# A hybrid decoder block with product-key experts on one core: operands of the gate products kept token by token

## The chip, the cores and the metric

The kernel runs on one core of one Trainium2 chip, in one launch. The metric is device time in microseconds (us), from the start to the end of one execution; a few executions are timed and the median is quoted. One further execution is recorded by the hardware profiler, and the rows below come from that one. Engines are called as the profile calls them: PE (TensorE, matmuls), PEld (the weight loads of PE), DVE (VectorE), ACT (ScalarE), POOL (GpSimd) and SP (SyncE, which here issues DMAs).

## The reference

One decoder layer on 512 tokens of width 1024: modulation from `c`, an attention group (8 query heads, window 128, sinks) beside a gated short convolution, an output projection, and then a product-key expert layer, which takes most of the time. Cut to that layer:

```python
q  = (xt @ wq).reshape(T, 8, 2, 128)
sc = einsum('thpd,hpkd->thpk', q, subkeys)          # 8 heads, two halves, 128 keys
vals, ids = lax.top_k(sc, 16)                       # per half
cand = vals[..0, :, None] + vals[..1, None, :]      # 256 candidates a head
top, pos = lax.top_k(cand, 16)
idx = take(ids0 * 128 + ids1, pos);  g = softmax(top)
for tokens in chunks of 128:                        # u, v: 16384 x 1024 each
    a   = einsum('chkd,cd->chk', u[idx], x)
    out = einsum('chk,chkd->cd', g * gelu(a), v[idx])
```

Each token thus picks 128 of 16384 experts (8 heads, 16 each), every one of which is a row of `u` and a row of `v` of 1024 floats. An expert's number is 128 i + j, with i and j from 0 to 127.

## The kernel before

**Two ways through the experts.** Of the 512 tokens, 384 (`TD`) are worked densely: all 16384 experts are multiplied out on PE, 128 at a time (one slice j holds the 128 experts of all i), and those that a token did not pick get gate zero. The last 128 tokens gather their rows of `u` and `v` by indirect DMAs on POOL and take dot products and sums on DVE (`gathered`, lines 771, 779, 894). 64 of the 384 dense tokens (`HT`) gather their rows of `u` too (`last_dense`), so that the first dense product has 320 columns (`TU`).

**First product (`first`, line 608 on).** For slice j the table `uL[j]` (512 KB) is loaded, split into two reduced-precision parts by ACT (`hi`, line 174) and DVE (`lo`, line 175), and multiplied in 24 matmuls of 320 columns (lines 198 to 200); ACT writes the gelu (line 619). Results of the first 64 slices (`SPILL`) go to DRAM, a pair of slices at a time (`Ad`, 320 KB), and come back as `sp`. Those of the other slices wait on the chip, in `RING` = 5 buffers `ge` of one pair each.

**Gates (`build`, lines 903 to 944).** The dense gates of 16 tokens are built at a time, in 24 builds. For each token, PE multiplies a 128x128 matrix A (row = one of the token's 128 picks, 1 where i matches) with B (row = pick, value = gate where j matches), once for the gate's upper part (B1, line 938) and once for its lower (B2, line 939). The product is the token's 128x128 map of gates. DVE makes A by comparing with an iota (line 926), and B as the product of two smaller matrices, H (the upper three bits of j) and L1 or L2 (the lower four bits, times the gate; lines 920 to 923 and 930). H, L, L1 and L2 are made for two builds at once. The operands are float16, in tiles laid out [4 groups][128 columns][4 tokens]: the 128 columns of one token lie 4 elements apart, and four neighbouring elements belong to four tokens. A matmul of one token reads `A[:, b, :, t]` and `B1[:, b, :, t]`. Four tokens share a PSUM bank, which ACT writes to `st` (line 941); after two builds `st` goes to DRAM (`Gd`, 2 MB).

**The loop around it.** Each build of the first 16 is followed by two `first` and three steps of `last_dense` (a row to fetch and a dot product on DVE); the last 8 builds by one `first` each. Then come the `first` still missing up to slice 72, and then the main loop over the 128 slices: `gated` loads the gates of 8 slices from `Gd` (`G`), multiplies them with the first product (line 963) and splits the result; `second` multiplies with `vL[j]` (18 matmuls of 512 columns, lines 980 to 982) into six PSUM banks that stay open to the end; from slice 64 on each slice has a further `first`. Steps of `gathered` are taken between, as many as `PACE` allows (1.85 us a slice before slice `SPILL`, 4.4 us from it on).

**What sets the order.** Every engine works its own queue in order; a scheduler puts the program's instructions into the queues by the order in which it is written and by data dependences. A tile with one or two buffers makes its writer wait for the readers of the earlier contents: A, B1 and B2 have two buffers, H, L, L1 and L2 one.

Of the kernel before, what the change touches and what calls it, by code (L numbers as in the profile page):

```python
# [9 lines left out]
F16 = mybir.dt.float16  # L10
# [3 lines left out]
AF = mybir.ActivationFunctionType  # L14
OP = mybir.AluOpType
# [3 lines left out]
P = 128  # L19
# [5 lines left out]
TD = ND * P  # L25
# [7 lines left out]
TB = 32  # L33
NB = TD // TB
GS = 32768.0
RING = 5
LOOK = 4
SPILL = 64
EARLY = 1
STB = 2  # L40
LD = 5
# [48 lines left out]
def body(tc, p):  # L90
    nc = tc.nc
    es = ExitStack()

    def pool(name, bufs=1, **kw):
        st = ExitStack()
        return st.enter_context(tc.tile_pool(name=name, bufs=bufs, **kw)), st

    cp, cp_s = pool("cp")
# [11 lines left out]
    def bank(name):  # L110
        return psm.tile([P, 512], F32, tag="m", name=name)
# [21 lines left out]
    nc.vector.memset(eps, EPS)  # L133
    eps64 = cp.tile([P, 1], F32, name="eps64")
    nc.vector.memset(eps64, 64 * EPS)
    iotaX = cp.tile([P, P, 4], F16, name="iotaX")
    nc.vector.tensor_copy(iotaX, C("iota")[:, :, None].to_broadcast([P, P, 4]))
    iotaA = cp.tile([P, 16, 16], F16, name="iotaA")
    nc.vector.tensor_copy(iotaA, C("iota")[:, 0:16, None].to_broadcast([P, 16, 16]))

# [336 lines left out]
    for step in PLAN.split():  # L477
        n = [int(x) for x in step[1:]]
# [75 lines left out]
    pp, pp_s = pool("pp")  # L554
    h2H = pp.tile([P, DC, TU], F32R, name="h2H")
    h2L = pp.tile([P, DC, TU], F32R, name="h2L")
    iT = pp.tile([P, TD], F16, name="iT")
    jhT = pp.tile([P, TD], F16, name="jhT")
    jlT = pp.tile([P, TD], F16, name="jlT")
    g1T = pp.tile([P, TD], F16, name="g1T")  # L560
    g2T = pp.tile([P, TD], F16, name="g2T")
    h2N = pp.tile([P, D], F32, name="h2N")
    hN = pp.tile([P, D], F32, name="hN")
    eH = pp.tile([P, HT], I32, name="eH")
# [18 lines left out]
    for r, (dst, cs) in enumerate(((hN, slice(TU - HT, TD)), (h2N, slice(TD, T)))):  # L583
        pg = [bank("pg0"), bank("pg1")]
        for k in range(DC):
            b = mod[:, 24 + k:25 + k]
# [15 lines left out]
    rp, rp_s = pool("rp", side="right")  # L602
    Ad = dp.tile([SPILL // 2, P, 2, TU], F32, name="Ad")
    ring = {}
    lead = [0]

    def first():
        j = lead[0]
        if j == NJ:
            return  # L610
        lead[0] += 1
        w = weights_of(p["uL"][j])
        ps = psa.tile([P, TU], F32, tag="a", name="pa")
        mm3(ps, w, lambda k: h2H[:, k, :], lambda k: h2L[:, k, :])
        m, i = divmod(j, 2)
        if i == 0:
            ring[m] = up.tile([P, 2, TU], F32, name="sp", bufs=3) if j < SPILL else \
                rg.tile([P, 2, TU], F32, name="ge", bufs=RING)
        nc.scalar.activation(ring[m][:, i], ps, AF.Gelu_apprx_tanh)  # L619
        if i and j < SPILL:  # L620
            nc.sync.dma_start(Ad[m], ring.pop(m))
# [201 lines left out]
    for c in range(ND):  # L823
# [11 lines left out]
        n = P if c < ND - 1 else P - HT  # L835
# [65 lines left out]
    stage, low = [None], [None]  # L901

    def build(bt):

        ts_ = slice(bt * 16, (bt + 1) * 16)

        def tok(x, w, ts):
            n = (ts.stop - ts.start) // 4
            return x[:, ts].rearrange("p (b t) -> p b t", t=4)[:, :, None, :].to_broadcast([P, n, w, 4])

        def iotas(step, w, n):
            return iotaX[:, None, 0:step * w:step, :].to_broadcast([P, n, w, 4])

        def tile_(name, n, w):
            return gb.tile([P, n, w, 4], F16, tag=name, name=name, bufs=1 if n == 8 else 2)

        if bt % 2 == 0:
            t2 = slice(bt * 16, (bt + 2) * 16)
            H, L, L1, L2 = [tile_(x, 8, w) for x, w in (("H", 8), ("L", 16), ("L1", 16), ("L2", 16))]
            nc.vector.tensor_tensor(H, iotas(16, 8, 8), tok(jhT, 8, t2), op=OP.is_equal)  # L920
            nc.vector.tensor_tensor(L, iotas(1, 16, 8), tok(jlT, 16, t2), op=OP.is_equal)
            nc.vector.tensor_mul(L1, L, tok(g1T, 16, t2))
            nc.vector.tensor_mul(L2, L, tok(g2T, 16, t2))
            low[0] = H, L1, L2
        A, B1, B2 = [tile_(x, 4, P) for x in ("A", "B1", "B2")]
        nc.vector.tensor_tensor(A, iotas(1, P, 4), tok(iT, P, ts_), op=OP.is_equal)
        bs = slice((bt % 2) * 4, (bt % 2) * 4 + 4)
        sh = [P, 4, 8, 16, 4]
        for B, L in ((B1, low[0][1]), (B2, low[0][2])):
            nc.vector.tensor_mul(B.rearrange("p b (h l) t -> p b h l t", h=8),  # L930
                                 low[0][0][:, bs, :, None, :].to_broadcast(sh), L[:, bs, None, :, :].to_broadcast(sh))
        if bt % 2 == 0:
            stage[0] = gb.tile([P, NJ, TB], F32, tag="st", name="st", bufs=STB)
        for b in range(4):
            ps = bank("gps")
            for t in range(4):
                o = ps[:, t * P:(t + 1) * P]
                nc.tensor.matmul(o, A[:, b, :, t], B1[:, b, :, t], start=True, stop=False)  # L938
                nc.tensor.matmul(o, A[:, b, :, t], B2[:, b, :, t], start=False, stop=True)  # L939
            t0 = (bt % 2) * 16 + b * 4  # L940
            nc.scalar.activation(stage[0][:, :, t0:t0 + 4], ps.rearrange("p (t j) -> p j t", t=4), AF.Copy,
                                 scale=1.0 / GS)
        if bt % 2:
            nc.sync.dma_start(Gd[bt // 2], stage[0])

    def gated(m):

        if 2 * m < SPILL:
            a = up.tile([P, 2, TU], F32, name="sp", bufs=3)
# [52 lines left out]
    gb, gb_s = pool("gb")  # L1002
# [110 lines left out]
```

## Time and profile before

| | us |
|---|---|
| median of 3 runs | 1490.91 (1484.22 to 1491.93) |
| the profiled execution | 1482.77 |
| its span, first to last instruction | 1481.0 |
| PE busy, in the span | 1414.3 |
| PEld busy | 1236.0 |
| DVE busy | 1268.3 |
| ACT busy | 613.8 |
| POOL busy | 439.2 |
| the 24 builds, first to last gate matmul | 480.4 to 703.5 |
| main loop, first multiplication of gates | 722.6 |

The profiled execution is 8.1 us shorter than the median of the timed runs. A matmul's row shows its start and a modelled length that overlaps the next one; how fast PE goes is therefore read from the distance of two starts, not from the length. [...] DMA is the mean busy share of the 16 DMA engines.

### The profile page before, as it was taken

What the parts mean: (1) busy time and instruction counts of PE and PEld (TensorE: products, weight loads), DVE (VectorE), ACT (ScalarE), POOL (GpSimd) and SP (SyncE); (2) the same over time, 40 slices, a digit from 0 to 9 for tenths busy, and PEclk for the clock granted to TensorE, in tenths of its full rate; (3) what the DMA queues carried; (4) which work ended last, traced back from release to release, by engine and by line L of the source; (5) the groups of instructions that cost most, each with busy time, mean ns of one, the idle gap of its engine ahead of it and who ended that gap; (6) DMA issues with size and microseconds to landing.
All of it is one profiled execution on the core that took longest, in us unless ns stands there. A gap on an engine that the chain in (4) does not pass through costs nothing.

```text
span 1481.0 us, 21313 instructions
## 1 busy us (share of the span) xinstructions
PE 1414.3 (95%) x7696; PEld 1236.0 (83%) x7696; DVE 1268.3 (86%) x2330; ACT 613.8 (41%) x1029; POOL 439.2 (30%) x324
## 2 busy tenths in 40 slices
PE   6999998999896999999999999998999999999998
PEld 4776776788896999999977888887888999888986
DVE  7777978899997899869789788887979999888984
ACT  4533546433632444544434433343333343433341
POOL 0000000000154033300122344454766655555600
PEclk9999999999998999999999999999999999999999
DMA  8644535232699599977898999999999999999963
GB/s 293 222 160 152 182 128 181 83 95 76 193 358 350 211 347 380 364 280 258 298 377 290 353 377 394 403 370 350 356 393 356 408 401 388 401 347 379 372 216 128
DMA packets 138282, 432.07 MB, mean 292 GB/s; under 512 B 13120, under 2 KB 39872, under 8 KB 136640
## 3 DMA queue, kind: packets, MB, share of 16 engines
q1 hardware_dynamic: 92096, 262.92, 49.3%
q0 software_dynamic: 46080, 167.79, 30.0%
q8 instruction: 60, 0.98, 0.3%
q14 instruction: 46, 0.38, 0.1%
HBM read 390.78 MB, written 39.85 MB: 291 GB/s over the span
## 4 chain that ended last, share of the span: by engine, by line
PE 23%; issue 9%; DMA 9%; DVE 7%; POOL 4%; ACT 0%; DVEq 0%; POOLq 0%
PE o L982 6%; PE o L981 5%; PE o L980 5%; DMA row<-in_uR,eG 4%; POOL row L771 4%; DMA row<-in_vL,eG 4%; PE pa L198 2%; PE pa L200 2%; PE pa L199 2%; DVE lo L175 2%; DVE ga L894 2%; DVE junk L779 1%; DVE wwl L175 1%; DVE x L999 0%; PE gps L939 0%
## 5 line engine op out<-in xcount | busy, mean ns | idle before, releaser
L174 ACT ACTIVATE hi<-raw 128x1024 fp32r<-128x1024 f32 x298 | 312.2, 1054 | 330.6 <-PE pa L199 153.5
L175 DVE TENSOR_TENSOR lo<-raw,hi 128x1024 fp32r<-128x1024 f32 x298 | 362.7, 1219 | 43.7 <-ACT hi L174 40.9
L198 PE MATMUL pa<-h2H,hi 128*128 128x320 f32 x1024 | 320.9, 313 | 17.8 <-ACT sp L619 17.8
L200 PE MATMUL pa<-h2H,lo 128*128 128x320 f32 x1024 | 320.2, 313 | 5.5 <-DVE lo L175 5.5
L199 PE MATMUL pa<-h2L,hi 128*128 128x320 f32 x1024 | 318.9, 311 | 0.0
L981 PE MATMUL o<-lo,wwh 128*128 128x512 f32 x768 | 301.4, 392 | 7.9 <-DVE lo L175 7.9
L982 PE MATMUL o<-hi,wwl 128*128 128x512 f32 x768 | 300.6, 391 | 4.5 <-DVE wwl L175 4.4
L980 PE MATMUL o<-hi,wwh 128*128 128x512 f32 x768 | 300.9, 392 | 0.0
L771 POOL DMA_INDIRECT row<-in_uR,eG x128 | 181.8, 1420 | 297.4 <-PE o L982 139.5
L771 POOL DMA_INDIRECT row<-in_uR,eH x64 | 83.0, 1298 | 553.9 <-DVE eq L690 407.2
L198 PEld LDWEIGHTS pa<-h2H,hi 128*128 128x128 f32 x1024 | 194.7, 190 | 21.7 <-ACT sp L619 19.5
L771 POOL DMA_INDIRECT row<-in_vL,eG x128 | 174.2, 1361 | 122.1 <-DVE ga L894 67.9
L779 DVE SCALAR_TENSOR_TENSOR junk<-row,h2N 128x1024 bf16<-128x1024 f32 x128 | 153.5, 1220 | 59.0 <-DMA row<-in_uR,eG 58.6
L200 PEld LDWEIGHTS pa<-h2H,lo 128*128 128x128 f32 x1024 | 194.3, 190 | 7.0 <-DVE lo L175 7.0
L199 PEld LDWEIGHTS pa<-h2L,hi 128*128 128x128 f32 x1024 | 194.4, 190 | 2.2
L894 DVE SCALAR_TENSOR_TENSOR ga<-row,av,ga 128x1024 f32<-128x1024 f32 x127 | 163.1, 1284 | 19.7 <-DMA row<-in_vL,eG 18.2
L981 PEld LDWEIGHTS o<-lo,wwh 128*128 128x128 f32 x768 | 144.8, 188 | 38.8 <-DVE lo L175 10.5
L982 PEld LDWEIGHTS o<-hi,wwl 128*128 128x128 f32 x768 | 144.8, 189 | 37.5 <-DVE wwl L175 7.3
L980 PEld LDWEIGHTS o<-hi,wwh 128*128 128x128 f32 x768 | 144.7, 188 | 28.4 <-issue 0.2
L962 ACT ACTIVATE w<-G 128x64 f32<-128x64 f32 x128 | 25.8, 249 | 322.7 <-DVE wwl L175 322.6
L938 PE MATMUL gps<-B,A 128*128 128x128 f16 x384 | 90.8, 297 | 1.6 <-DVE B L930 1.6
L939 PE MATMUL gps<-B,A 128*128 128x128 f16 x384 | 89.3, 298 | 0.0
(263 smaller groups left out, 1918.4 us busy)
## 6 DMA issues: line engine op xcount, KB each, us to landing
raw<-in_uL SPq DMA_DIRECT2D x128, 512.0 KB, 6.8
raw<-in_vL SPq DMA_DIRECT2D x128, 512.0 KB, 7.1
Gd<-st SPq DMA_DIRECT2D x12, 2048.0 KB, 8.5
G<-Gd SPq DMA_DIRECT2D x16, 1536.0 KB, 16.1
ada<-in_ada SPq DMA_DIRECT2D x32, 512.0 KB, 4.3
Ad<-sp SPq DMA_DIRECT2D x32, 320.0 KB, 5.5
sp<-Ad SPq DMA_DIRECT2D x32, 320.0 KB, 7.3
raw<-in_w_in SPq DMA_DIRECT2D x18, 512.0 KB, 5.3
```

The costliest lines, as they stand in the source:

```text
L174: nc.scalar.activation(h, f, AF.Copy)
L175: nc.vector.tensor_sub(l, f, h.bitcast(F32))
L198: nc.tensor.matmul(ps, wh(k), rh(k), start=(k == k0), stop=False)
L199: nc.tensor.matmul(ps, wh(k), rl(k), start=False, stop=False)
L200: mark[0] = nc.tensor.matmul(ps, wl(k), rh(k), start=False, stop=(k == k1))
L771: d = nc.gpsimd.indirect_dma_start(out=t, out_offset=None, in_=tab, in_offset=bass.IndirectOffsetOnAxis(ap=e, axis=0))
L779: nc.vector.scalar_tensor_tensor(junk, t, 1.0, h, op0=OP.mult, op1=OP.mult, accum_out=a)
L894: nc.vector.scalar_tensor_tensor(ga, t, av[:, k:k + 1], ga, op0=OP.mult, op1=OP.add)
L938: nc.tensor.matmul(o, A[:, b, :, t], B1[:, b, :, t], start=True, stop=False)
L980: nc.tensor.matmul(o, wh[:, cs], vh[:, hs], start=(j == 0), stop=False)
L981: nc.tensor.matmul(o, wh[:, cs], vl[:, hs], start=False, stop=False)
L982: last = nc.tensor.matmul(o, wl[:, cs], vh[:, hs], start=False, stop=(j == NJ - 1))
```

## The change

The tiles A, B1 and B2 get the layout [16 tokens][128 columns], so that a matmul reads one token's 128 columns side by side: `A[:, 4*b + t]`. For DVE to go on with four equal neighbours in a row, the five token vectors (i, the two parts of j, the two parts of the gate) now lie in one tile `slots`, and once per two builds ACT copies 32 tokens of all five into a new tile `x` of 5 x 32 x 4 elements, each value four times (line 907). DVE compares and multiplies from `x`. H is now [32 tokens][8][4], each value four times: 1024 elements a partition where it had 256. The iota over [128][4] is replaced by two smaller ones. `x` has one buffer.

The tile `x` and the larger H take room; `RING` goes from 5 to 4, and `SPILL` from 64 to 66, so that one more pair of slices goes through DRAM and the pace of the gathered steps changes at slice 66. The number of slices whose first product is done before the main loop is 72 in both (`SPILL + 2*RING - 2`).

```diff
-RING = 5
+RING = 4
-SPILL = 64
+SPILL = 66
...
-    iotaX = cp.tile([P, P, 4], F16, name="iotaX")
+    iota1 = cp.tile([P, 32, 4], F16, name="iota1")
+    nc.vector.tensor_copy(iota1.rearrange("p a b -> p (a b)"), C("iota"))
+    iotaH = cp.tile([P, 8, 4], F16, name="iotaH")
...
+    slots = pp.tile([P, 5, TD], F16, name="slots")
+    iT, jhT, jlT, g1T, g2T = (slots[:, k] for k in range(5))
...
+            x = gb.tile([P, 5, 32, 4], F16, name="x", bufs=1)
+            nc.scalar.activation(x, slots[:, :, t2, None].to_broadcast([P, 5, 32, 4]), AF.Copy)
+            H = gb.tile([P, 32, 8, 4], F16, name="H", bufs=1)
+            L, L1, L2 = [gb.tile([P, 32, 4, 4], F16, name=n, bufs=1) for n in ("L", "L1", "L2")]
...
-        nc.vector.tensor_tensor(A, iotas(1, P, 4), tok(iT, P, ts_), op=OP.is_equal)
+        nc.vector.tensor_tensor(A.rearrange("p t (a b) -> p t a b", b=4), iota1[:, None].to_broadcast(sA),
+                                x[:, 0, ts, None].to_broadcast(sA), op=OP.is_equal)
+        sh = [P, 16, 8, 4, 4]
+        for B, L in ((B1, L1), (B2, L2)):
+            nc.vector.tensor_mul(B.rearrange("p t (h a b) -> p t h a b", h=8, a=4),
+                                 H[:, ts, :, None, :].to_broadcast(sh), L[:, ts, None].to_broadcast(sh))
...
-                nc.tensor.matmul(o, A[:, b, :, t], B1[:, b, :, t], start=True, stop=False)
-                nc.tensor.matmul(o, A[:, b, :, t], B2[:, b, :, t], start=False, stop=True)
+                nc.tensor.matmul(o, A[:, 4 * b + t], B1[:, 4 * b + t], start=True, stop=False)
+                nc.tensor.matmul(o, A[:, 4 * b + t], B2[:, 4 * b + t], start=False, stop=True)
```

In DVE's queue, at a change from one pair of builds to the next in the middle of the builds, this stands before (junk is a dot product of `last_dense`, lo the split of a weight slice):

```order
L779 SCALAR_TENSOR_TENSOR junk,aH<-row,hN 128x1024
L175 TENSOR_TENSOR lo<-raw,hi 128x1024
L779 SCALAR_TENSOR_TENSOR junk,aH<-row,hN 128x1024
L175 TENSOR_TENSOR lo<-raw,hi 128x1024
L779 SCALAR_TENSOR_TENSOR junk,aH<-row,hN 128x1024
L920 TENSOR_TENSOR H<-iotaX,jhT 128x256
L921 TENSOR_TENSOR L<-iotaX,jlT 128x512
L926 TENSOR_TENSOR A<-iotaX,iT 128x2048
L922 TENSOR_TENSOR L_6053<-L,g1T 128x512
L923 TENSOR_TENSOR L_6054<-L,g2T 128x512
L930 TENSOR_TENSOR B_6060<-H,L_6053 128x2048
L930 TENSOR_TENSOR B_6061<-H,L_6054 128x2048
```

and this now, at the same place:

```order
L778 SCALAR_TENSOR_TENSOR junk,aH<-row,hN 128x1024
L177 TENSOR_TENSOR lo<-raw,hi 128x1024
L778 SCALAR_TENSOR_TENSOR junk,aH<-row,hN 128x1024
L177 TENSOR_TENSOR lo<-raw,hi 128x1024
L778 SCALAR_TENSOR_TENSOR junk,aH<-row,hN 128x1024
L912 TENSOR_TENSOR H<-iotaH,x 128x1024
L914 TENSOR_TENSOR L<-iota_96,x 128x512
L923 TENSOR_TENSOR A<-iota_96,x 128x2048
L916 TENSOR_TENSOR L_6067<-L,x 128x512
L917 TENSOR_TENSOR L_6068<-L,x 128x512
L927 TENSOR_TENSOR B_6074<-H,L_6067 128x2048
L927 TENSOR_TENSOR B_6075<-H,L_6068 128x2048
```

The order of the instructions is the same; H is four times as wide, and H, L, A, L1 and L2 read `x` where they read the token vectors.

In ACT's queue, among the first builds, this stands before (hi is the split of a weight slice, sp the gelu of a first product, st the writing out of gate maps):

```order
L941 ACTIVATE st<-gps 128x128x4 x4
L174 ACTIVATE hi<-raw 128x1024
L619 ACTIVATE sp<-pa 128x320
L174 ACTIVATE hi<-raw 128x1024
L619 ACTIVATE sp<-pa 128x320
L941 ACTIVATE st<-gps 128x128x4 x4
L174 ACTIVATE hi<-raw 128x1024
L619 ACTIVATE sp<-pa 128x320
L174 ACTIVATE hi<-raw 128x1024
L619 ACTIVATE sp<-pa 128x320
L941 ACTIVATE st<-gps 128x128x4 x4
```

and this now:

```order
L938 ACTIVATE st<-gps 128x128x4 x4
L907 ACTIVATE x<-slots 128x640
L176 ACTIVATE hi<-raw 128x1024
L618 ACTIVATE sp<-pa 128x320
L176 ACTIVATE hi<-raw 128x1024
L618 ACTIVATE sp<-pa 128x320
L938 ACTIVATE st<-gps 128x128x4 x4
L176 ACTIVATE hi<-raw 128x1024
L618 ACTIVATE sp<-pa 128x320
L907 ACTIVATE x<-slots 128x640
L176 ACTIVATE hi<-raw 128x1024
L618 ACTIVATE sp<-pa 128x320
```

One copy into `x` is added for every two builds; it stands ahead of a split hi, which waits behind it.

## Rows read from the trace of the kernel before

**Rows 1.** The page's GB/s line: what the DMA engines moved in each of 40 equal slices of the span.

```profile
GB/s 293 222 160 152 182 128 181 83 95 76 193 358 350 211 347 380 364 280 258 298 377 290 353 377 394 403 370 350 356 393 356 408 401 388 401 347 379 372 216 128
```

**Rows 2.** Busy time of the engines in eleven stretches that cover the builds. Columns: stretch and its length in us, then busy us and number of instructions of PE, PEld, DVE, ACT and POOL, then the granted clock of PE, DMA's busy share, and GB/s.

```profile
476.00:500.00 24.00, 22.11 (x155) 21.20 (x156) 23.42 (x30) 11.19 (x19) 1.08 (x1) 0.81 0.52 197
500.00:520.00 20.00, 20.00 (x152) 19.69 (x150) 14.71 (x19) 9.50 (x15) 2.61 (x2) 1.00 0.73 264
520.00:540.00 20.00, 20.00 (x149) 19.71 (x147) 18.05 (x24) 8.90 (x14) 7.23 (x6) 1.00 0.95 350
540.00:560.00 20.00, 20.00 (x149) 19.70 (x147) 18.82 (x26) 8.55 (x14) 6.33 (x6) 1.00 0.98 372
560.00:580.00 20.00, 20.00 (x151) 19.80 (x149) 18.35 (x24) 9.77 (x16) 6.18 (x6) 1.00 0.96 358
580.00:600.00 20.00, 20.00 (x151) 19.69 (x150) 18.05 (x25) 9.26 (x15) 6.57 (x6) 1.00 0.99 370
600.00:620.00 20.00, 20.00 (x151) 19.68 (x150) 18.05 (x25) 9.55 (x16) 7.23 (x6) 1.00 1.00 376
620.00:640.00 20.00, 20.00 (x151) 19.68 (x150) 15.68 (x23) 10.10 (x16) 6.29 (x5) 1.00 0.98 377
640.00:660.00 20.00, 20.00 (x151) 19.68 (x150) 16.65 (x23) 8.71 (x14) 0.00 (x0) 1.00 0.60 224
660.00:680.00 20.00, 20.00 (x150) 19.26 (x149) 13.15 (x33) 9.98 (x17) 0.00 (x0) 1.00 0.70 273
680.00:704.00 24.00, 22.50 (x176) 21.58 (x176) 24.00 (x67) 12.49 (x22) 0.00 (x0) 0.93 0.72 250
```

**Rows 3.** PE's instructions in order of time: start us, length us. Gate matmuls of one build (from the first row to the second are seven steps, on lines 938 and 939 in turn), matmuls of a first product (sixteen steps), and of a second product (eighteen steps).

```profile
540.19 0.30 PE L939 MATMUL gps<-B,A 128*128 128x128 f16 x1
...
541.02 0.30 PE L938 MATMUL gps<-B,A 128*128 128x128 f16 x1
...
542.33 0.31 PE L199 MATMUL pa<-h2L,hi 128*128 128x320 f32 x1
...
544.67 0.31 PE L200 MATMUL pa<-h2H,lo 128*128 128x320 f32 x1
...
801.25 0.39 PE L980 MATMUL o<-hi,wwh 128*128 128x512 f32 x1
...
805.33 0.39 PE L980 MATMUL o<-hi,wwh 128*128 128x512 f32 x1
```

**Rows 4.** The same view at the start of the builds, two first-product matmuls on PE and three weight loads of gate matmuls on PEld.

```profile
478.01 0.47 PE L198 MATMUL pa<-h2H,hi 128*128 128x320 f32 x1
478.28 0.47 PE L199 MATMUL pa<-h2L,hi 128*128 128x320 f32 x1
480.39 0.34 PEld L938 LDWEIGHTS <-A 128*128 128x128 f16 x3 [1.63 <-issue]
```

**Rows 5.** The same view, earlier in the kernel: two of nine transposes of 128 columns of float32, which follow one another, on PE; and twelve weight loads of 128 columns of float32 on PEld, for matmuls of two columns.

```profile
458.78 0.27 PE L826 MATMUL ijg<-cst,Ri 128*128 128x128 f32 x1
458.89 0.27 PE L826 MATMUL ijg<-cst,Rj 128*128 128x128 f32 x1
...
55.51 1.58 PEld L355 LDWEIGHTS ssq<-cs,sq 128*128 128x128 f32 x12 [1.27 <-ACT sq L353]
```

**Rows 6.** Groups of instructions, the first five in the stretch from 476 to 704 us, the last two in the whole span. Columns: line, engine, operation, out<-in with partitions x elements and type, count | busy us, mean ns of one | idle us before them and who ended it.

```profile
L926 DVE TENSOR_TENSOR A<-iotaX,iT 128x2048 f16<-128x2048 f16 x24 | 29.3, 1221 | 11.2 <-PE gps L939 11.2
L175 DVE TENSOR_TENSOR lo<-raw,hi 128x1024 fp32r<-128x1024 f32 x39 | 47.4, 1221 | 11.1 <-ACT hi L174 8.8 <-PE gps L939 2.3
L920 DVE TENSOR_TENSOR H<-iotaX,jhT 128x256 f16<-128x256 f16 x12 | 3.5, 288 | 0.0
L198 PE MATMUL pa<-h2H,hi 128*128 128x320 f32 x298 | 94.9, 318 | 11.1 <-ACT sp L619 11.1
L941 ACT ACTIVATE st<-gps 128x512 f32<-128x512 f32 x96 | 57.2, 596 | 29.3 <-PE gps L939 19.6 <-issue 9.2 <-ACT sp L619 0.3
L690 DVE TENSOR_TENSOR eq<-eq 128x1024 f16<-128x1024 f16 x6 | 4.1, 683 | 0.0
L666 ACT ACTIVATE ex<-I 128x1024 f16<-128x1024 uint32 x4 | 4.2, 1049 | 0.1
```

**Rows 7.** Waits by pairs from 475 to 595 us: who waited for whom, us in total, times, longest us.

```profile
POOL row L771 <- DVE junk L779: 90.4, 24, 36.2
ACT hi L174 <- PE pa L199: 48.0, 20, 2.8
```

**Rows 8.** Busy time in the stretch of the main loop in which first and second products alternate (columns as in rows 2); and the page's line on the DMA that brings a spilled pair back: count, KB each, median us to landing.

```profile
960.00:1440.00 480.00, 467.84 (x2505) 417.17 (x2504) 427.64 (x450) 177.38 (x277) 271.77 (x191) 0.99 0.97 366
sp<-Ad SPq DMA_DIRECT2D x32, 320.0 KB, 7.3
```

**Rows 9.** PE in order of time behind two waits, start us and length us, the wait before in brackets.

```profile
799.53 0.50 PE L982 MATMUL o<-hi,wwl 128*128 128x512 f32 x1 [1.65 <-DVE wwl L175]
799.87 0.40 PE L980 MATMUL o<-hi,wwh 128*128 128x512 f32 x1
...
1331.65 0.64 PE L200 MATMUL pa<-h2H,lo 128*128 128x320 f32 x1 [2.65 <-DVE lo L175]
1332.08 0.47 PE L198 MATMUL pa<-h2H,hi 128*128 128x320 f32 x1
```

More of the change, by code (lines that the diff above doesn't have):

```diff
@@ L135, in body @@
     nc.vector.memset(eps64, 64 * EPS)
-    iotaX = cp.tile([P, P, 4], F16, name="iotaX")
-    nc.vector.tensor_copy(iotaX, C("iota")[:, :, None].to_broadcast([P, P, 4]))
+    iota1 = cp.tile([P, 32, 4], F16, name="iota1")
+    nc.vector.tensor_copy(iota1.rearrange("p a b -> p (a b)"), C("iota"))
+    iotaH = cp.tile([P, 8, 4], F16, name="iotaH")
+    nc.vector.tensor_copy(iotaH, C("iota")[:, 0:P:16, None].to_broadcast([P, 8, 4]))
     iotaA = cp.tile([P, 16, 16], F16, name="iotaA")
@@ L556, in body @@
     h2L = pp.tile([P, DC, TU], F32R, name="h2L")
[L557 to L561, printed above, removed]
+    slots = pp.tile([P, 5, TD], F16, name="slots")
+    iT, jhT, jlT, g1T, g2T = (slots[:, k] for k in range(5))
     h2N = pp.tile([P, D], F32, name="h2N")
@@ L903, in build @@
     def build(bt):
[L905 to L915, printed above, removed]
         if bt % 2 == 0:
@@ L918, in build @@
             t2 = slice(bt * 16, (bt + 2) * 16)
[L919 to L925, printed above, removed]
@@ L926, in build @@
-        nc.vector.tensor_tensor(A, iotas(1, P, 4), tok(iT, P, ts_), op=OP.is_equal)
[L927 to L931, printed above, removed]
+            x = gb.tile([P, 5, 32, 4], F16, name="x", bufs=1)
+            nc.scalar.activation(x, slots[:, :, t2, None].to_broadcast([P, 5, 32, 4]), AF.Copy)
@@ new lines, in build @@
+            H = gb.tile([P, 32, 8, 4], F16, name="H", bufs=1)
+            L, L1, L2 = [gb.tile([P, 32, 4, 4], F16, name=n, bufs=1) for n in ("L", "L1", "L2")]
+            sl = [P, 32, 4, 4]
+            sH8 = [P, 32, 8, 4]
+            nc.vector.tensor_tensor(H, iotaH[:, None].to_broadcast(sH8), x[:, 1, :, None].to_broadcast(sH8),
+                                    op=OP.is_equal)
+            nc.vector.tensor_tensor(L, iota1[:, None, 0:4].to_broadcast(sl), x[:, 2, :, None].to_broadcast(sl),
+                                    op=OP.is_equal)
@@ new lines, in build @@
+            nc.vector.tensor_mul(L1, L, x[:, 3, :, None].to_broadcast(sl))
+            nc.vector.tensor_mul(L2, L, x[:, 4, :, None].to_broadcast(sl))
+            low[0] = x, H, L1, L2
+        x, H, L1, L2 = low[0]
+        ts = slice((bt % 2) * 16, (bt % 2) * 16 + 16)
+        A, B1, B2 = [gb.tile([P, 16, P], F16, name=n, bufs=2) for n in ("A", "B1", "B2")]
+        sA = [P, 16, 32, 4]
+        nc.vector.tensor_tensor(A.rearrange("p t (a b) -> p t a b", b=4), iota1[:, None].to_broadcast(sA),
+                                x[:, 0, ts, None].to_broadcast(sA), op=OP.is_equal)
```

## The prediction

> **What bounds the kernel now.** I read the page first and then the stretches, because only one stage is changed. In the 24 builds, from 480 to 704 us, the reader is to see in [rows 2] that PE is busy in every microsecond of 500 to 680, at full clock, and that two others are close behind: DVE works 18.0 to 18.8 of every 20 us from 520 to 620 and all of the last 24 us, and the DMA engines are busy for 0.95 to 1.00 of the time from 520 to 640. The waits say the same from the other side [rows 7]: ACT waits 48.0 us for PE before it splits a weight slice, and POOL 90.4 us for DVE's dot products before it may fetch another row. So the stage is PE's by a small margin, and what a faster PE is worth is read from the idle time of DVE and DMA.
>
> PE's time there has two parts. Gate matmuls start 0.83 / 7 = 0.119 us apart, with 128 columns each; the 320-column matmuls of the first product start 2.34 / 16 = 0.146 us apart, the 512-column ones of the second 4.08 / 18 = 0.227 us apart [rows 3]. The last two lie on a line: 0.080 us for 192 columns more, and 0.013 us that does not depend on columns. On that line 128 columns take 0.053 + 0.013 = 0.066 us. The gate matmuls are thus nearly twice as slow as their columns. Nor does the array's clock pace them: at the start of the builds, where the first product goes at 0.27 us a matmul (the lower level), the loads of three gate matmuls take 0.34 us, 0.113 each [rows 4]. What is left is the reading of operands that lie four elements apart, which the change alters.
>
> **The change part by part.** *Gate matmuls.* 24 builds of 32 are 768. At 0.066 us instead of 0.119, PE saves 768 x 0.053 = 40 us. No row shows a load of 128 float16 columns side by side, so this is bounded: above by nothing saved, because twelve loads of 128 float32 columns side by side take 1.58 us, 0.13 each, and transposes of 128 columns side by side start 0.11 apart [rows 5]; below by the 40 us. I take the 40: the float32 rows have twice the bytes, and the rows that are nearest, the float16 ones, keep their 0.113 to 0.119 at either clock level, which points at the reading.
>
> [...]
>
> *What of the 40 us is worth time.* In a 20 us stretch PE would save 40 / 228 x 20 = 3.5 us. DVE's order is unchanged, so its idle time is the most that a stretch can lose. DVE gets H with 1024 elements instead of 256: 0.683 instead of 0.288 us [rows 6], 12 times, 4.7 us, 0.4 in 20 us. From [rows 2], the smaller of 3.5 and DVE's idle time less 0.4: 476 to 500 0.1; 500 to 520 3.5; the five stretches to 620 1.95 + 1.18 + 1.65 + 1.95 + 1.95 - 2.0 = 6.7; 620 to 640 3.5; 640 to 660 2.9; 660 to 680 3.5; 680 to 704, where DVE is full, -0.5. That is 19.7 us. If a busy share of 1.00 were the end of what DMA can do, the stretches from 520 to 640 could lose only their free shares, 0.14 x 20 = 2.8 instead of 10.2 us, and the sum would be 12.3. But the page has slices with 401 to 408 GB/s [rows 1] where these move 350 to 377, so I leave nearly all of it: 18 us. The most is all of DVE's idle time, 29.1 - 4.7 = 24.4.
>
> *The copy into x.* 640 elements lie between 512 in 0.596 us and 1024 in 1.049 us [rows 6]; by the line between, 0.71 us, 12 times, 8.5 us on ACT, which is busy for 108 of these 228 us. It waits for DVE's last reader of the old x, the A of the pair's second build; behind it in ACT's queue stand a split hi and the writing out of gate maps, and DVE's lo waits for hi. Cover: after that A, DVE still makes two B of 1.2 us and mostly dot products and splits before the next H, and hi has 48.0 us of waiting for PE to give away. Bounds: nothing, and 8.5 us if DVE stands through each copy. I take 0.5. *DVE's other operations* have the same element counts and still four neighbours in a row: no change taken; if the new patterns ran slower by a tenth, A and B would cost 8 us, if faster, as much would be gained. *The smaller iotas* are outside the builds, under 0.5 us.
>
> *RING and SPILL.* One pair more is written and read back: 2 x 128 x 2 x 320 x 4 bytes = 0.66 MB. Where it is read DMA is busy for 0.97 at 366 GB/s [rows 8]: 1.8 us; nothing if it hides. SP gets one DMA of each kind, a landing of 7.3 us that is asked for ahead. The first product stays 72 slices ahead at the start and runs two slices later from slice 66; the steps of `gathered` lose 2 x 2.55 us before slice 66 and catch up. PE's work is unchanged by this; I take 0, bounds in the first rival.
>
> *Sum.* -18 + 0.5 + 1.8 = -15.7, say -16 us. What follows the builds starts earlier by as much. The profiled execution, 1482.77 us, would become 1467; the median before is 8.1 us higher, and 1490.9 - 16 = 1475 us is the forecast.
>
> **The rivals.**
> First: the main loop gives it back. Speaking for it: DMA is at 0.97 there and PE still idles 480.0 - 467.8 = 12.2 us [rows 8], so that it is near two limits; with rows arriving a little later and one pair less on the chip, DVE may wait more for rows and PE for DVE. Against: the lead of the first product over the use of its buffer is the same. If PE's 12.2 us double: 1475 + 12 = 1487 us.
>
> Second: the weight load, not the distance of the elements, paces the pair, as the float32 rows at 0.11 to 0.13 allow [rows 5]. Then 0 to 7 us are saved on PE (768 x 0.009), and x, H and the spilled pair cost up to 4: 1484 to 1495, say 1490 us.
>
> Third, on the other side: PE, which now has to wait for DVE between builds, falls to the lower clock. Behind a wait of 1.65 us it went on at the upper level, a 512-column matmul of 0.40 us; behind one of 2.65 us a 320-column matmul has the length 0.47 us of the lower level [rows 9]. The place is the change from pair to pair of builds, where DVE has H, L, A, L1, L2 and two B to make before PE gets a gate. The lower level lasted from 476.3 to past 481 us at the start [rows 4], so a fall costs some 3 us of work, and 2.65 of waiting. PE would need 228 - 40 = 188 us plus 5.65 for each fall; from 7 of the 12 pairs on it is slower than now. With 10: 244.5, 16.5 more than 228, and 2.3 for the rest: 1510 us. Against: the time that PE gets to spare is 40 - 18 = 22 us, 1.8 a pair if it is not split further, less than 2.65.
>
> **How the numbers follow.** Forecast 0.65 (1467 to 1481 by the bounds of DVE and DMA), first rival 0.11, second 0.16, third 0.08. A measurement of this kernel tells about 0.5%, 7.5 us, from no change, so faster means below 1483.5. The forecast is all faster; of the first rival 0.02 is faster and 0.01 slower; of the second 0.02 and 0.03; of the third 0.07 slower. Faster 0.69, same 0.20, slower 0.11. The range goes from 1463, somewhat beyond DVE's whole idle time, to 1492, over the first rival and most of the second; it leaves out the third.
>
> **What would show it.** Right: the gate matmuls start 0.06 to 0.08 us apart, the builds take 200 to 212 us instead of 223, DVE idles under 15 us in them, A no longer waits for PE (11.2 us [rows 6]), and PE waits for DVE's B. H 0.68 us, x 0.7. [...]

## The result and the profile after

The changed kernel takes 1464.03 us (median of 4 runs, 1463.03 to 1467.20); before, on the same chip, takes 1487.57 us (median of 4, 1483.55 to 1491.93). The ratio is 0.986, 95% interval 0.9834 to 0.9886: 17 to 25 us less. The profiled execution of the changed kernel is its 1467.2 us one, with a span of 1465.2 us. A profile shows one execution: this one is the longest of its four, and that of before, 1482.77 us, is shorter than all four timed here, so that the two profiles differ by 15.6 us and the medians by 23.5.

The first thing to look at is the gate matmuls, in PE's instructions in order of time, the view of [rows 3] (start us, length us):

```profile
544.18 0.22 PE L936 MATMUL gps<-B,A 128*128 128x128 f16 x1
...
544.85 0.22 PE L936 MATMUL gps<-B,A 128*128 128x128 f16 x1
```

Between the two rows lie twelve steps: 0.67 / 12 = 0.056 us, where it was 0.119. How long the builds take is read from the same view summed by line: count, shortest/median/longest ns, first and last start. First before, then the changed kernel:

```profile
L938 PE MATMUL gps<-B,A x384: 277/297/302, 480.4 to 703.4; 128*128 128x128 f16 x192
L939 PE MATMUL gps<-B,A x384: 285/298/330, 482.5 to 703.5; 128*128 128x128 f16 x192
```

```profile
L935 PE MATMUL gps<-B,A x384: 216/219/314, 482.1 to 674.4; 128*128 128x128 f16 x192
L936 PE MATMUL gps<-B,A x384: 216/219/311, 483.3 to 674.5; 128*128 128x128 f16 x192
```

From the first gate matmul to the last: 223.1 us before, 192.4 now, 30.7 less. The stretches of [rows 2] show what sets the end of the builds now (stretch and length in us; busy us and count of PE, PEld, DVE, ACT, POOL; granted clock, DMA share, GB/s):

```profile
500.00:520.00 20.00, 20.00 (x194) 19.80 (x192) 20.00 (x26) 12.34 (x22) 4.51 (x3) 1.00 0.92 329
520.00:540.00 20.00, 20.00 (x177) 19.80 (x176) 19.36 (x26) 10.93 (x19) 9.56 (x6) 1.00 1.01 385
540.00:560.00 20.00, 20.00 (x178) 19.80 (x177) 20.00 (x27) 11.45 (x19) 9.55 (x6) 1.00 1.02 416
560.00:580.00 20.00, 19.92 (x176) 19.49 (x175) 20.00 (x27) 10.32 (x18) 9.58 (x6) 1.00 1.02 400
580.00:600.00 20.00, 18.60 (x160) 17.63 (x160) 20.00 (x28) 11.18 (x19) 9.58 (x6) 1.00 1.03 413
600.00:620.00 20.00, 18.85 (x164) 17.85 (x163) 19.08 (x26) 9.59 (x16) 9.55 (x6) 1.00 1.01 387
620.00:640.00 20.00, 16.08 (x158) 14.43 (x156) 20.00 (x27) 10.55 (x20) 3.36 (x2) 1.00 0.98 396
640.00:660.00 20.00, 17.40 (x151) 16.49 (x151) 19.60 (x49) 8.95 (x16) 0.00 (x0) 1.00 0.74 266
660.00:680.00 20.00, 17.59 (x161) 16.30 (x159) 20.00 (x51) 11.57 (x20) 0.00 (x0) 0.83 0.64 243
```

DVE and PE have changed places. DVE is busy in nearly every microsecond, and PE has idle time from 580 us on. DMA, which moved 350 to 377 GB/s in the middle of the builds, now moves 385 to 416. The groups of instructions from 476 to 704 us, the answer to [rows 6] (busy us, mean ns | idle us before them and who ended it), show the same from DVE's side: A waits for nobody, where it waited 11.2 us for PE.

```profile
L923 DVE TENSOR_TENSOR A<-iota,x 128x2048 f16<-128x2048 f16 x24 | 29.1, 1214 | 0.0
L912 DVE TENSOR_TENSOR H<-iotaH,x 128x1024 f16<-128x1024 f16 x12 | 8.2, 682 | 0.0
...
L907 ACT ACTIVATE x<-slots 128x640 f16<-128x640 f16 x12 | 8.9, 745 | 15.0 <-DVE A L923 11.8 <-DVE slots L806 3.2
```

The waits by pairs from 475 to 595 us, which answer to [rows 7]: ACT waited 48.0 us for PE, and now waits 27.3; POOL's rows still wait for DVE's dot products.

```profile
POOL row L770 <- DVE junk L778: 76.5, 27, 31.5
ACT hi L176 <- PE pa L201: 27.3, 13, 5.0
```

Not all of the 30.7 us arrives at the end. In these two profiles the first matmul of the second product starts 29.1 us earlier (698.9 instead of 728.0 us), the last one only 15.3 us earlier (1460.2 instead of 1475.5). First before, then the changed kernel:

```profile
L980 PE MATMUL o<-hi,wwh x768: 388/389/798, 728.0 to 1475.0; 128*128 128x512 f32 x192
L982 PE MATMUL o<-hi,wwl x768: 387/389/628, 728.5 to 1475.5; 128*128 128x512 f32 x192
```

```profile
L977 PE MATMUL o<-hi,wwh x768: 387/389/792, 698.9 to 1459.8; 128*128 128x512 f32 x192
L979 PE MATMUL o<-hi,wwl x768: 387/389/632, 699.4 to 1460.2; 128*128 128x512 f32 x192
```

The main loop has become 13.8 us longer in this pair of profiles, and most of this is time in which PE waits. From 1000 to 1400 us, first before and then the changed kernel (columns as above):

```profile
1000.00:1400.00 400.00, 387.84 (x2102) 347.55 (x2101) 356.82 (x371) 145.55 (x227) 240.59 (x170) 0.99 1.00 377
```

```profile
1000.00:1400.00 400.00, 377.70 (x2036) 336.88 (x2035) 345.55 (x350) 138.88 (x218) 231.41 (x164) 0.98 0.97 364
```

PE's idle time there has gone from 12.2 to 22.3 us; all but 0.2 us of it ends, in both profiles, with DVE's lo, the split of a weight slice. Two explanations were open. Either the main loop cannot use a head start, because DMA and DVE are nearly full there (a share of 1.00 and 356.8 of 400 us before) whatever happens ahead of it; or the other half of the change, RING 4 and SPILL 66, costs this time by itself. Open as well was which of the two operands had paced the gate matmul, A, which is loaded, or B, which is streamed, and whether DVE really is the new bound.

### The profile page after: what moved, and what is told of

It reads as the page before. It is cut to its first block, busy times and chain, and to the rows that moved or that the text cites. A ratio compares the mean times of both kernels' runs of the same rounds, so it can differ in the third digit from the quotient of the medians.

```text
span 1465.2 us, 21360 instructions
## 1 busy us (share of the span) xinstructions
PE 1379.4 (94%) x7696; PEld 1196.9 (82%) x7696; DVE 1270.6 (87%) x2331; ACT 615.8 (42%) x1041; POOL 451.8 (31%) x324
## 4 chain that ended last, share of the span: by engine, by line
PE 43%; DVE 26%; DMA 13%; issue 11%; POOL 4%; ACT 2%; SPq 0%; DVEq 0%; POOLq 0%; ACTq 0%
DVE lo L177 6%; DMA row<-in_uR,eG 6%; PE o L978 5%; PE o L979 5%; PE o L977 5%; POOL row L770 4%; PE pa L202 4%; PE pa L200 4%; PE pa L201 4%; DVE junk L778 3%; DMA row<-in_vL,eG 3%; DMA row<-in_uR,eH 3%; PE pj L200 2%; PE pj L202 2%; PE pj L201 2%
## 5 line engine op out<-in xcount | busy, mean ns | idle before, releaser
L177 DVE TENSOR_TENSOR lo<-raw,hi 128x1024 fp32r<-128x1024 f32 x298 | 362.1, 1217 | 34.8 <-ACT hi L176 29.3
L200 PE MATMUL pa<-h2H,hi 128*128 128x320 f32 x1024 | 321.8, 314 | 16.5 <-ACT sp L618 16.5
L202 PE MATMUL pa<-h2H,lo 128*128 128x320 f32 x1024 | 321.1, 314 | 12.1 <-DVE lo L177 11.8
L770 POOL DMA_INDIRECT row<-in_uR,eG x128 | 173.4, 1354 | 286.2 <-PE o L979 122.6
L770 POOL DMA_INDIRECT row<-in_uR,eH x64 | 97.9, 1529 | 527.8 <-DVE eq L689 405.3
L770 POOL DMA_INDIRECT row<-in_vL,eG x128 | 180.3, 1409 | 132.5 <-DVE ga L893 79.7
L200 PEld LDWEIGHTS pa<-h2H,hi 128*128 128x128 f32 x1024 | 195.4, 191 | 20.2 <-ACT sp L618 17.8
L202 PEld LDWEIGHTS pa<-h2H,lo 128*128 128x128 f32 x1024 | 195.1, 191 | 15.3 <-DVE lo L177 15.3
L778 DVE SCALAR_TENSOR_TENSOR junk<-row,hN 128x1024 bf16<-128x1024 f32 x64 | 77.6, 1215 | 17.1 <-DMA row<-in_uR,eH 16.6
L176 ACT ACTIVATE wwh<-w 128x768 fp32r<-128x768 f32 x64 | 53.8, 841 | 65.0 <-PE o L978 61.4
```

Source lines behind the costliest of these rows:

```text
L176: nc.scalar.activation(h, f, AF.Copy)
L177: nc.vector.tensor_sub(l, f, h.bitcast(F32))
L200: nc.tensor.matmul(ps, wh(k), rh(k), start=(k == k0), stop=False)
L202: mark[0] = nc.tensor.matmul(ps, wl(k), rh(k), start=False, stop=(k == k1))
L770: d = nc.gpsimd.indirect_dma_start(out=t, out_offset=None, in_=tab, in_offset=bass.IndirectOffsetOnAxis(ap=e, axis=0))
L778: nc.vector.scalar_tensor_tensor(junk, t, 1.0, h, op0=OP.mult, op1=OP.mult, accum_out=a)
```

## The experiments

Ratios are to the kernel before, run on the same chip.

**The ring half alone.** The kernel before with the two numbers of the change:

```diff
-RING = 5
+RING = 4
-SPILL = 64
+SPILL = 66
```

> Before with the second half of the change alone: RING 4 and SPILL 66, the old operands. Theory 'the ring costs little': gate matmuls stay 0.119 us apart, the builds take 223 us as before, and the time is within 4 us of before (0.997 to 1.003 of it; the 0.66 MB more at 366 GB/s are 1.8 us). Rival 'the ring is what the main loop gives back' (about 14 us were given back there between 1040 and 1400 us in the profile of the changed kernel): 8 to 14 us more than before, ratio 1.005 to 1.010.

Measured: 1495.21 us, 1.0059 (1.0037 to 1.008). The rival has the number right: RING 4 and SPILL 66 cost 5 to 12 us with the builds as they were. The gate matmuls are the old ones, and from the first to the last it takes 223.2 us. The time is lost in the main loop, where PE idles nearly as long as in the changed kernel (1000 to 1400 us):

```profile
1000.00:1400.00 400.00, 379.41 (x2035) 338.10 (x2034) 342.59 (x360) 140.91 (x220) 234.57 (x165) 0.98 0.98 365
```

PE idles 20.6 us. Of this 15.1 us are waits of the second product for DVE's lo, before 7.9, in the changed kernel 15.2; first here, then before, then the changed kernel:

```profile
PE o L981 <- DVE lo L175: 15.1, 8, 6.3
```

```profile
PE o L981 <- DVE lo L175: 7.9, 7, 4.6
```

```profile
PE o L978 <- DVE lo L177: 15.2, 9, 5.1
```

Why lo comes late the profiles do not settle. ACT, which makes hi ahead of lo, waits 45.9 us for the first product's weights here and 9.8 us before, but only 14.2 us in the changed kernel; in the same order:

```profile
ACT hi L174 <- DMA raw<-in_uL: 45.9, 10, 13.2
```

```profile
ACT hi L174 <- DMA raw<-in_uL: 9.8, 5, 4.5
```

```profile
ACT hi L176 <- DMA raw<-in_uL: 14.2, 6, 3.9
```

**A alone token by token.** RING 4 and SPILL 66, the old layout of H, L and B, the new one of A:

```diff
-nc.vector.tensor_tensor(A, iotas(1, P, 4), tok(iT, P, ts_), op=OP.is_equal)
+A = gb.tile([P, 16, P], F16, name="A", bufs=2)
+nc.vector.tensor_tensor(A.rearrange("p t (a b) -> p t a b", b=4), iota1[:, None].to_broadcast(sA),
+                        low[0][3][:, xs, None].to_broadcast(sA), op=OP.is_equal)
...
-nc.tensor.matmul(o, A[:, b, :, t], B1[:, b, :, t], start=True, stop=False)
+nc.tensor.matmul(o, A[:, 4 * b + t], B1[:, b, :, t], start=True, stop=False)
```

> RING 4 and SPILL 66, with A alone (the operand that is loaded) token by token and B as before, four elements apart. If the load of A set the old distance of 0.119 us: 0.056 to 0.066 now, and builds near 195 us. If the streaming of B set it: 0.119 still, builds 223 us, the time as in the ring-only run. If each of the two takes 0.11 by itself and they overlap: 0.11 to 0.12, nothing gained. If they add up: about 0.088, builds near 205 us.

**B alone token by token.** The changed kernel with the old A:

```diff
-                nc.tensor.matmul(o, A[:, 4 * b + t], B1[:, 4 * b + t], start=True, stop=False)
...
+                nc.tensor.matmul(o, A[:, b, :, t], B1[:, 4 * b + t], start=True, stop=False)
```

> The changed kernel with A built as before, four elements apart, and B alone token by token. If the load of A set the old distance: 0.11 to 0.119, builds near 223 us. If the streaming of B set it: 0.056 to 0.066, builds near 195 us and a time near that of the changed kernel (0.986 of before). If each takes 0.11 by itself and they overlap: 0.11 to 0.12 here and in the run with A alone. If they add up: about 0.088 in both.

Measured: with A alone 1495.47 us, 1.0053 (1.0026 to 1.008), the same as the ring half alone; with B alone 1460.0 us, 0.9834 (0.9807 to 0.9862), the same as the whole change within the intervals. PE in order of time, A alone, eight steps between the rows:

```profile
539.75 0.29 PE L947 MATMUL gps<-B,A 128*128 128x128 f16 x1
...
540.68 0.30 PE L947 MATMUL gps<-B,A 128*128 128x128 f16 x1
```

And B alone, twelve steps:

```profile
540.21 0.22 PE L939 MATMUL gps<-B,A 128*128 128x128 f16 x1
...
540.88 0.22 PE L939 MATMUL gps<-B,A 128*128 128x128 f16 x1
```

That is 0.93 / 8 = 0.116 us against 0.67 / 12 = 0.056. The operand that is streamed set the pace, and the spacing of the loaded one costs nothing that can be seen: in the run with B alone the load of the strided A is recorded at 115 ns, longer than the 56 ns between matmuls, and is hidden all the same.

```profile
L940 PEld LDWEIGHTS <-A 128*128 128x128 f16 x384 | 42.0, 115 | 0.4
```

**More work for DVE.** The changed kernel with B2 multiplied out a second time:

```diff
-for B, L in ((B1, L1), (B2, L2)):
+for B, L in ((B1, L1), (B2, L2), (B2, L2)):
```

> The changed kernel with B2 multiplied out twice in each build: 24 x 1.21 = 29 us more for DVE and nothing for PE or DMA. Theory 'the builds are now bound by DVE' (226 of 228 us busy): they take 25 to 29 us longer, 218 to 222 instead of 193. Rival 'PE or DMA ends them': under 8 us longer. For the whole: if the main loop gives half of the builds' gain back, 12 to 17 us over the changed kernel, a ratio of 0.994 to 0.998 to before; if it gives nothing back, 25 to 29 us, a ratio of 1.003 to 1.006.

Measured: 1485.4 us, 0.9991 (0.9972 to 1.001). The builds, first gate matmul to last, take 219.3 us (486.5 to 705.8), 26.9 more than the changed kernel's 192.4, for 29 us of work on DVE. DVE is the bound of the builds. To the end 0.9991 - 0.986 = 0.0131 arrives, some 19 us, between the two figures that were expected for the whole; with two intervals of 0.002 to 0.003 how much the main loop gives back is not settled by it. The stretches show something else that the third rival spoke of: PE, with more idle time, is granted a mean clock of 0.91 in six of the eleven from 500 to 720 us.

```profile
540.00:560.00 20.00, 16.53 (x138) 15.64 (x137) 20.00 (x28) 8.84 (x15) 7.86 (x5) 0.91 0.93 343
...
640.00:660.00 20.00, 14.74 (x122) 13.12 (x121) 20.00 (x25) 9.23 (x15) 3.37 (x2) 0.91 0.85 328
```

**Which of the two numbers.** SPILL alone, RING alone, and both with the pace of rows and dot products switched where it was; all with the builds of before:

```diff
-SPILL = 64
+SPILL = 66
```

> Before with RING 5 as it was and SPILL 66 alone: one spilled pair more, the first product taken up again two slices later in the main loop, and the dot products at their slow pace for two slices more (2 x 2.55 us of their steps later). The ring-only run (both numbers) was 1.0059 of before. Theory 'the later switch costs it' (the pace, the spilled pair, or both): 1.004 to 1.007 here too, and with RING 4 alone nothing. Theory 'the fewer waiting pairs cost it': 0.998 to 1.002 here.

```diff
-RING = 5
+RING = 4
```

> Before with RING 4 alone, SPILL 64 as it was: the first product is 70 slices ahead instead of 72 when the main loop begins, and 6 to 8 instead of 8 to 10 pairs' slices wait in the loop. Theory 'the fewer waiting pairs cost it': 1.004 to 1.007 of before, with PE idle some 20 us instead of 12 from 1000 to 1440. Theory 'the later switch costs it': 0.998 to 1.002.

```diff
-            todo += PACE[j >= SPILL]
+            todo += PACE[j >= 64]
```

> The ring-only kernel (RING 4, SPILL 66) with the pace of the dot products and rows switched at slice 64 as before, so that they are no longer 2 x 2.55 us late. If the pace is what costs: 0.998 to 1.002 of before instead of the ring-only run's 1.0059. If it is the spilled pair, the later first product or the ring: 1.004 to 1.008 still.

Measured: SPILL 66 alone 1502.52 us, 1.0117 (1.0085 to 1.015). RING 4 alone 1489.39 us, 1.0021 (0.9999 to 1.0044), not told from before. Both, with the old switch of the pace, 1490.13 us, 1.0022 (0.9996 to 1.0047). So SPILL 66 costs by itself, and RING 4 by itself at most 0.0044. Two slices more at the slow pace seem to be most of it when RING is 4: without them 0.0037 of the 0.0059 is gone, but the two intervals overlap, so this is indicated and not shown. PE's idle time in a single profile does not decide it: it is 18.2 us with RING 4 alone, near what the theory of the fewer waiting pairs had said, and 17.3 us with the old switch, in two kernels whose times are not told from before. Nor does ACT's wait for the first product's weights, which is still 44.2 us with the old switch. SPILL 66 alone cost more than I had expected from any of the theories; with RING 5 it also puts two more first products ahead of the main loop (74 instead of 72), and the second product starts 5.0 us later in its profile (733.0 us). How its 17 us divide between that, the pace and the spilled pair was not tried.

**The same on the changed kernel.** RING 4 kept, SPILL put back:

```diff
-SPILL = 66
+SPILL = 64
```

> The changed kernel with RING 4 but SPILL 64, as before: 70 slices of first products ahead, and the pace of rows and dot products switched at slice 64. Theory 'the ring half of the change costs time in the main loop whatever the builds do': the difference of the ring-only run to the run with RING 4 alone (1.0059 to 1.0021) comes back here as well, 0.980 to 0.984 of before against 0.986 of the changed kernel, 1456 to 1462 us. Rival 'with the shorter builds the main loop gives the head start back anyway': 0.985 to 0.988.

Measured: 1456.28 us, 0.9791 (0.976 to 0.9822). What SPILL costs comes back here too, 0.0069 or some 10 us, slightly more than was expected; the rival, a main loop that gives back any head start, would have left it at 0.985 or more. The builds take 190.1 us here (486.6 to 676.7), 33.0 less than before, and 31 us of that arrive at the end.

**Two copies instead of four.** The changed kernel asks for memory because x, H and the iota rows hold each value four times. Two neighbours, and L2 written over L, leave room for RING 5 and SPILL 64:

```diff
-RING = 4
+RING = 5
-SPILL = 66
+SPILL = 64
...
-x = gb.tile([P, 5, 32, 4], F16, name="x", bufs=1)
+x = gb.tile([P, 5, 32, 2], F16, name="x", bufs=1)
...
-H = gb.tile([P, 32, 8, 4], F16, name="H", bufs=1)
-L, L1, L2 = [gb.tile([P, 32, 4, 4], F16, name=n, bufs=1) for n in ("L", "L1", "L2")]
+H = gb.tile([P, 32, 8, 2], F16, name="H", bufs=1)
+L, L1 = [gb.tile([P, 32, 8, 2], F16, name=n, bufs=1) for n in ("L", "L1")]
+L2 = L
```

> The changed kernel with two copies of each value side by side in x, H, L and the iota rows instead of four, L2 written over L, and with the memory that this frees RING 5 and SPILL 64 again. If DVE needs only two neighbours to keep its rate: A and B 1.21 us, H 0.41 (512 elements as L has), and the ring's cost of the ring-only run (0.6%, 8.8 us) comes back: 0.976 to 0.981 of before, 1449 to 1456 us. If DVE needs four: A and B near 2.2 us, 72 us more for DVE in the builds, and a time over 1500 us, 1.01 to 1.04 of before.

Measured: 1452.14 us, 0.978 (0.9747 to 0.9813). This is not told from the run before it, 0.9791 with four copies, RING 4 and SPILL 64: no run shows that the room for RING 5 is needed. DVE keeps its rate with two neighbours; its groups from 476 to 704 us:

```profile
L928 DVE TENSOR_TENSOR B<-H,L 128x2048 f16<-128x2048 f16 x48 | 56.5, 1218 | 0.0
...
L924 DVE TENSOR_TENSOR A<-iota,x 128x2048 f16<-128x2048 f16 x24 | 29.1, 1212 | 0.0
...
L913 DVE TENSOR_TENSOR H<-iotaH,x 128x512 f16<-128x512 f16 x12 | 4.9, 412 | 0.0
```

And in the main loop PE idles no longer than before (10.6 us), although it starts 34.8 us earlier (693.2 us):

```profile
1000.00:1400.00 400.00, 389.41 (x2115) 349.72 (x2114) 361.41 (x363) 146.27 (x230) 231.56 (x163) 0.99 0.98 368
```

This kernel with the change's two numbers tells the layout from the ring:

```diff
-RING = 5
+RING = 4
-SPILL = 64
+SPILL = 66
```

> The two-wide kernel with RING 4 and SPILL 66, the change's numbers. Theory 'the two-wide kernel's gain over the changed one is mostly the ring': 0.983 to 0.986 of before (0.978 plus 0.6%, less nothing). Rival 'it is the shorter H and x' (12 x 0.27 us of DVE): 0.978 to 0.981.

Measured: 1462.26 us, 0.9831 (0.9805 to 0.9857), at the lower edge of what was expected if the ring is most of it, and 0.005 behind the two-wide kernel. Over the changed kernel the smaller H and x alone are at most a few us.

**The pace.** The runs on SPILL point at the rows and dot products of the main loop, so the second pace was lowered in the two-wide kernel, and then in the kernel before:

```diff
-PACE = (1.85, 4.4)
+PACE = (1.85, 4.1)
```

> The two-wide kernel with the second pace 4.1 instead of 4.4: rows and dot products spread over some four slices more at the end, where DMA moves only 126 to 305 GB/s in the last 80 us, and 7% fewer of them in each slice before, where DMA is at 0.96 to 1.03. If DMA's share is what PE's idle time of 1000 to 1400 (10.6 us in the two-wide kernel's profile) hangs on: 2 to 7 us less, 0.973 to 0.977 of before. If not, or if the end now waits for the rows: 0.978 to 0.985.

> Before with the second pace 4.1 instead of 4.4 and nothing else. The two-wide kernel gained 0.8% by it. Theory 'it is a matter of the main loop alone, where rows and dot products ask for more than DMA gives': 0.990 to 0.995 of before here too, 8 to 14 us. Rival 'only the earlier start of the main loop, after the shorter builds, made the slower pace the better one': 0.998 to 1.004.

Measured: two-wide 1443.07 us, 0.9699 (0.9675 to 0.9723), the fastest kernel of this study; before 1473.28 us, 0.9933 (0.9908 to 0.9958). Some 10 us in both, so the gain does not hang on the shorter builds. In the profile of the second, an execution of 1463.91 us, PE idles 6.1 us from 1000 to 1400, half of before's 12.2:

```profile
1000.00:1400.00 400.00, 393.95 (x2159) 354.21 (x2158) 354.80 (x367) 148.44 (x230) 218.84 (x162) 1.00 0.99 372
```

In the profile of the two-wide kernel with the new pace, an execution of 1450.6 us, PE idles 9.9 us against 10.6, so that there the gain is seen in the times only. That fewer rows a slice leave DMA more room for the weights does not fit the waits: from 1000 to 1400 us ACT waits longer for weights with the new pace, 35.2 + 11.7 us instead of 13.2 + 9.8. First before, then with the new pace:

```profile
ACT hi L174 <- DMA raw<-in_vL: 13.2, 7, 5.4
ACT hi L174 <- DMA raw<-in_uL: 9.8, 5, 4.5
```

```profile
ACT hi L174 <- DMA raw<-in_vL: 35.2, 8, 8.2
ACT hi L174 <- DMA raw<-in_uL: 11.7, 7, 4.4
```

PE's waits for DVE's lo fall from 12.1 to 5.9 us all the same. Whether that comes from the work of those rows on DVE or from something else, no run has shown.

A table puts the profiles beside each other. The main loop is taken from the first start of a second-product matmul to the last, PE's idle time from 1000 to 1400 us:

| kernel | RING, SPILL | main loop, us | length, us | PE idle, us |
|---|---|---|---|---|
| before | 5, 64 | 728.0 to 1475.5 | 747.5 | 12.2 |
| ring half alone | 4, 66 | 731.7 to 1492.6 | 760.9 | 20.6 |
| A alone | 4, 66 | 726.8 to 1488.4 | 761.6 | 18.2 |
| ring half, old switch of the pace | 4, 66 | 722.7 to 1476.9 | 754.2 | 17.3 |
| SPILL alone | 5, 66 | 733.0 to 1490.3 | 757.3 | 20.2 |
| RING alone | 4, 64 | 725.7 to 1485.3 | 759.6 | 18.2 |
| the change | 4, 66 | 698.9 to 1460.2 | 761.3 | 22.3 |
| B alone | 4, 66 | 695.3 to 1448.4 | 753.1 | 17.9 |
| change, B2 twice | 4, 66 | 728.9 to 1483.6 | 754.7 | 15.3 |
| change, SPILL 64 | 4, 64 | 699.4 to 1456.9 | 757.5 | 17.4 |
| two-wide | 5, 64 | 693.2 to 1444.4 | 751.2 | 10.6 |
| two-wide, RING 4, SPILL 66 | 4, 66 | 694.0 to 1455.3 | 761.3 | 17.9 |
| two-wide, new pace | 5, 64 | 697.9 to 1443.3 | 745.4 | 9.9 |
| before, new pace | 5, 64 | 721.6 to 1457.0 | 735.4 | 6.1 |

PE's idle time is 10 to 12 us with RING 5, SPILL 64 and the old pace, and 15 to 22 us with any other pair of numbers, whether the main loop begins near 693 or near 733 us; the kernels with RING 4 alone and with the old switch show that it does not always go with the time. The lengths of single profiles scatter by some us, but those that begin early are not longer as a group.

## Why the prediction was right, and where its steps were off

**The bound.** Right: PE ended the builds by a small margin, its faster matmuls were worth the idle time that DVE had, and DVE is the bound now: A no longer waits, and PE waits 8.1 us for DVE's B. Two of the signs that were named lie beyond their bands, the distance (0.056 us, named 0.06 to 0.08) and the builds (192.4 us, named 200 to 212).

**The gate matmul.** The direction was right, and what paced it was how an operand's elements lie, as argued: 0.056 us with B side by side, 0.116 with A alone so. The size was off: 0.056 us instead of the 0.066 of the line through the two wider matmuls, so PE saves 768 x 0.063 = 48 us, not 40. Of the line's 0.013 us that does not depend on columns only 0.056 - 0.053 = 0.003 is there for 128 float16 columns. The prediction also spoke of both operands; only the streamed one mattered. The load did not limit the pair: it is recorded at 100 to 101 ns in the changed kernel and at 115 with B alone, and matmuls with a load each start 56 ns apart in both. The second rival falls with the 56 ns.

```profile
L936 PEld LDWEIGHTS <-A 128*128 128x128 f16 x384 | 37.4, 101 | 0.6
L935 PEld LDWEIGHTS <-A 128*128 128x128 f16 x384 | 36.6, 100 | 12.8 <-issue 6.9 <-DVE B L927 4.3
```

**The builds.** Forecast 18 us less, at most 24.4; they are 30.7 us shorter. This is the first term that was mis-sized. Three steps made it small. I left 1.7 us to DMA, since a share of 1.00 looked like an end; at 1.01 to 1.03 DMA moved up to 416 GB/s. The sum let no stretch gain more than PE's 3.5 us, although DVE idled for longer in some (5.3 us from 500 to 520); from its first A to its last DVE took 213.9 us before and takes 188.6 now, 25.3 less where the sum had 19.7, close to all of its idle time, 24.4. And this was taken as the most, but the end of the builds is a gate matmul: before, the last gate matmul started 12.3 us behind DVE's last A (703.5 and 691.2 us), now 6.8 (674.5 and 667.7), and this smaller lag of PE gave the other 5.5. First before, then the changed kernel:

```profile
L926 DVE TENSOR_TENSOR A<-iotaX,iT x24: 1203/1224/1227, 477.3 to 691.2; 128x2048 f16<-128x2048 f16 x24
```

```profile
L923 DVE TENSOR_TENSOR A<-iota,x x24: 1206/1213/1221, 479.1 to 667.7; 128x2048 f16<-128x2048 f16 x24
```

**H, x and the other operations of DVE.** Right: H 0.682 us (0.683 forecast), x 0.745 (0.71), A 1.214 and B 1.212, as before (1.221 and 1.218). DVE's H has no wait for x in the changed kernel (0.0 us of idle time before it); ACT has the time, busy for 125.0 of the 228 us.

**RING and SPILL.** "I take 0" beside 1.8 us of DMA was wrong. It is the second mis-sized term, with the opposite sign: 8.8 us (5 to 12) measured alone. The step that failed is "the steps of `gathered` lose 2 x 2.55 us before slice 66 and catch up", taken as free: with the old switch of the pace most of the 8.8 us seems to be gone. How the later steps cost PE time is open. They are not made up for by a faster pace, since both kernels take 4.4 us of steps a slice from slice 66 on; they end about a slice later (2 x 2.55 / 4.4 = 1.2, an estimate). And later steps are not dear as such: a pace of 4.1 us a slice puts them off further and gains some 10 us. The first rival had the right place, nearly the right size (PE's 12.2 us of idle time about doubled) and, with rows that arrive later, a cause that the runs point at. What does not hold is a main loop that gives back any head start: the ring half costs its time with the old builds too, and with SPILL 64 nearly all that the builds gain arrives.

**The sum.** -30.7 + 8.8 = -21.9 us, against -23.5 by the medians and -16 forecast. The two errors, 12.7 and 7.0 us, lie on opposite sides and cancel in part. The forecast of 1475 us is 11 us too high; 3.3 of them lie in the median of before, 1490.9 us then and 1487.6 with a fourth run. The time is 1 us above the lower end of the range, 1463: without the 8.8 us of the ring half it would lie below it, as the changed kernel with SPILL 64 does (1456.3 us). That the range held is luck as much as mechanism.

**The third rival.** The lower level is a granted clock of 0.50 in the trace of before (from 476 to 485 us), the upper one 1.00. In the changed kernel the clock fell, after the first stretch (0.91 from 476 to 500 us, before 0.81), in one stretch of the builds only (0.83 from 660 to 680 us). With 29 us more work on DVE the mean was 0.91 in six stretches; the builds then took 219.3 us, still less than before, where the rival had priced 16.5 us more.

## What to carry to other kernels

When matmuls of few columns start much farther apart than the line through the wider ones allows (here 0.119 us against 0.066), look at the spacing of the streamed operand first, and keep its elements side by side (0.056 us here); the loaded operand can stay strided if another engine likes it so (0.056 us here too). When a change brings a second edit along to make room in memory, run that edit alone: here it cost 0.3 of what the main edit gained in the builds (8.8 of 30.7 us), and leaving SPILL at 64 would have spared it, with four copies and RING 4 (0.9791) as with two copies and RING 5 (0.978). Where PE, DVE and DMA are all nearly full, as in this main loop (before, from 1000 to 1400 us, PE busy for 387.8 and DVE for 356.8 us, DMA's share 1.00), the numbers that pace the work are worth trying again: 4.1 instead of 4.4 us a slice gained some 10 us in both kernels.

## What the runs showed of the hardware

Float16 matmuls of 128 columns start 0.116 to 0.119 us apart when the streamed operand's elements lie 8 bytes apart, and 0.056 us when they lie side by side. The loaded operand costs nothing that can be seen at a spacing of 8 bytes, although its load is recorded at 115 ns and the matmuls start 56 ns apart. DVE's float16 products and comparisons of 2048 elements take 1.21 to 1.22 us with runs of two neighbours as with runs of four. And a DMA share of 1.00 in a stretch of 20 us is no ceiling for bytes: 376 GB/s were moved at 1.00 before, 416 at 1.02 after.
